# Running sums of a 31-tap depthwise convolution: a PSUM tile in place of an SBUF tile

## The chip, the cores and the metric

One core of a Trainium2 chip runs the whole program. The metric is the device time of one execution in microseconds (us). A core has five engines with a queue each, which run their own instructions in order: TensorE (PE in the profile, its weight loads PEld), VectorE (DVE), ScalarE (ACT), GpSimd (POOL) and SyncE (SP, which issues the loads here). The engines wait for each other through semaphores. Tiles lie in SBUF or in PSUM, the memory that TensorE writes its products to.

## The reference, cut to what matters

The program is a two-layer decoder trunk over 272 positions of 2048 channels. Only the first mixer of layer 0 matters here:

```python
def causal_dwconv(x, w):
    K = w.shape[0]
    L = x.shape[1]
    xp = jnp.pad(x, ((0, 0), (K - 1, 0), (0, 0)))
    out = xp[:, 0:L] * w[0]
    for t in range(1, K):
        out = out + xp[:, t:t + L] * w[t]
    return out

def mixer_ab(h, w_in, conf_dw, conf_dw_b, conf_ln_g, conf_ln_b, sc_dw, w_out):
    z = h @ w_in
    a_val, a_gate, s_b, s_c, s_x = jnp.split(z, _splits(AB_SIZES), axis=-1)
    a = a_val * jax.nn.sigmoid(a_gate)
    a = causal_dwconv(a, conf_dw) + conf_dw_b
    a = jax.nn.silu(layernorm(a, conf_ln_g, conf_ln_b))
    s = s_b * causal_dwconv(s_c * s_x, sc_dw)
    return jnp.concatenate([a, s], axis=-1) @ w_out
```

`conf_dw` has 31 taps over 1024 channels, `sc_dw` 3 taps over 1024 channels. Everything is float32.

## The kernel before, in words

Activations are kept transposed: 128 channels on the partitions, 272 positions along the free dimension. A product with a float32 weight matrix is made column by column, a column being 128 output channels (`gemm`, `gemm_steps`, lines 138 to 166). For each column, weights come in blocks of 128x512 (`wf`). ScalarE rounds a block to `wh` (L152), and the rest `wl = wf - wh` is made by a subtraction (L154), on VectorE or, for the blocks listed in `pool_lo`, on GpSimd. TensorE then does three matmuls for each 128 rows of weights (L161, L162, L163), all into one PSUM tile `acc`. A column of the input projection has 2048 rows: four blocks, 48 matmuls. In this stage `pool_lo` is `PLO = (0, 1, 2)`: three of a column's four `wl` are made by GpSimd and the last by VectorE. There are two `acc` tiles, five `wh` and five `wl`.

The input projection has 40 columns. The first 16 are eight pairs (value, gate). Of each pair, VectorE scales the two products by `rstd` (L308 `av`, L305 `ag`), ScalarE applies a sigmoid, and VectorE multiplies them into the padded tile `ap` (L311). Then the convolution of these 128 channels runs as a generator, `conv_gen`: ScalarE writes the first tap and the bias into `c` (name `conv`, L278), and VectorE adds 30 taps one by one (L280), each reading the shifted `ap`, a scalar per partition from the parameter tile `par`, and the running sum `c`, and writing `c` again. GpSimd then adds the finished channel block into `csum` (L284, L286). The other 24 columns are eight groups of three (L325 `u`, L328 `u2`, L335 `sb`), with a 3-tap convolution (`conv3`, L235 to L237).

The taps are spread over the columns: after each column `run_taps(7)` lets the generators emit seven more taps, so the 240 taps stand between the columns' other VectorE instructions. A tap is also ordered behind the last `wl` of VectorE (`behind`). A scheduler then fixes the order of each engine's queue, which may interleave the taps of two channel blocks. TensorE needs VectorE's `wl` for the last quarter of every column.

Names in PSUM: `acc` is one of two buffers, `ps` one of six (`psb()`).

Of the kernel before, what the change touches and what calls it, by code (L numbers as in the profile page):

```python
# [12 lines left out]
AF = mybir.ActivationFunctionType  # L13
ALU = mybir.AluOpType
# [7 lines left out]
T = NM + SEQ  # L22
# [14 lines left out]
PAD = 48  # L37
OUT = NM - 2

# ---------------------------------------------------------------- layout of the packed parameters  # L40
_PAR = [
    ("norm_mix0", 16), ("eps", 1), ("norm_mix1", 16), ("norm_ffn0", 16), ("norm_ffn1", 16), ("norm_final", 16),
    ("conf_dw", 31 * 8), ("conf_b", 8), ("conf_g", 8), ("conf_bb", 8), ("sc_dw", 24),
# [48 lines left out]
def _body(ctx, tc, nc, A):  # L92
    V, S, G, PE = nc.vector, nc.scalar, nc.gpsimd, nc.tensor
# [13 lines left out]
    def pc(name, i=0, r0=0, r1=P):  # L107
        o = PO[name] + i
        return par[r0:r1, o:o + 1]
# [6 lines left out]
    def psb():  # L116
        return psB.tile([P, 512], F32, tag="ps", name="ps")

    def behind(ins, others):
        for o in others:  # L120
            tc.add_manual_dep(ins.ins, o.ins.name,
                              mybir.DependencyInfo(mybir.DependencyClass.NoSync, mybir.DependencyReason.DATA),
                              reason="activation tables")
# [6 lines left out]
        if last_hi[0] is not None:  # L130
            behind(w, [*last_hi, *after])

    # ---------------------------------------------------------------- products with split operands
    side = []
    def tick():
        for t in list(side):
# [39 lines left out]
    def parts(t, c0, c1):  # L176
        return t[:, 0, c0:c1], t[:, 1, c0:c1]

    # ---------------------------------------------------------------- residual stream and its norms
    h = []  # L180

    def inv_sqrt(dst, src, scale, eps, pool=None):
# [47 lines left out]
    def add_h(m, acc, c0):  # L230
        V.tensor_add(h[m][:, c0:], h[m][:, c0:], acc)  # L231

    # ---------------------------------------------------------------- causal short convolution
    def conv3(dst, src, n, wname, i):
        S.activation(dst, src[:, 0:n], AF.Copy, scale=pc(wname, 3 * i))  # L235
        V.scalar_tensor_tensor(dst, src[:, 1:1 + n], pc(wname, 3 * i + 1), dst, op0=ALU.mult, op1=ALU.add)
        V.scalar_tensor_tensor(dst, src[:, 2:2 + n], pc(wname, 3 * i + 2), dst, op0=ALU.mult, op1=ALU.add)  # L237

    # ---------------------------------------------------------------- mixer of layer 0
    def mixer_ab(tp):  # L240
        nm = Norm("norm_mix0", 0, tp)
        h0 = tp.tile([P, KD, T], F32, name="h0", bufs=1)
# [32 lines left out]
        PLO, NT = (0, 1, 2), 7  # L275

        def conv_gen(i, c, ap):
            S.activation(c, ap[:, 0:T], AF.Identity, scale=pc("conf_dw", 31 * i), bias=pc("conf_b", i))  # L278
            for t in range(1, 31):
                tap = V.scalar_tensor_tensor(c, ap[:, t:t + T], pc("conf_dw", 31 * i + t), c, op0=ALU.mult, op1=ALU.add)  # L280
                behind(tap, last_lo)
                yield
            if i == 0:
                G.tensor_copy(csum, c)  # L284
            else:
                G.tensor_add(csum, csum, c)  # L286
# [12 lines left out]
        for i in range(8):  # L299
# [9 lines left out]
            ap = tp.tile([P, T + 30], F32, tag="apad", name="ap", bufs=4)  # L309
            V.memset(ap[:, 0:30], 0.0)  # L310
            V.tensor_mul(ap[:, 30:], av, ag)  # L311
            c = tp.tile([P, T], F32, tag="conv", name="conv", bufs=8)
# [27 lines left out]
        run_taps(240)  # L340
        warm(AF.Sqrt)

        # layer norm over the channels
        a_split = []

        def ln_gen():
# [42 lines left out]
            nxt.feed(m)  # L389
        return nxt  # L390

    # ---------------------------------------------------------------- feed-forward
    def ffn(layer, nm, gname, c1, tp, feed, spill=None):
        nxt = Norm(gname, c1, tp)
        c0 = nm.c0
        n = T - c0
        pad = 2 if layer == 0 else 0
        no = n if layer == 0 else n - 2
        xs = nm.xs()
        up, down, dw = A["up%d" % layer], A["down%d" % layer], "ffn_dw%d" % layer  # L400
        for half in range(2):
            act = []
            for j in range(NFH):
                i = half * NFH + j
                res = []
                for q in range(2):
                    ps = gemm(up, 2 * i + q, xs, n)
                    nm.finish()
                    u = tp.tile([P, T + 2], F32, tag="u%d" % q, name="u")
                    if pad:  # L410
                        G.memset(u[:, 0:2], 0.0)  # L411
                    V.tensor_mul(u[:, pad:pad + n], ps, nm.rstd)  # L412
                    c = tp.tile([P, T], F32, tag="c%d" % q, name="c")
                    conv3(c[:, :no], u, no, dw, q * NF + i)
                    res.append(c[:, :no])
                silu = S.activation(res[1], res[1], AF.Silu)  # L416
                G.tensor_mul(res[0], res[0], res[1])  # L417
                d = tp.tile([P, 2, T], F32R, tag="act", name="act", bufs=24)
                split(d, res[0], no)
                act.append(parts(d, 0, no))  # L420
            warm(AF.Sqrt, [silu])
            for m in range(KD):
                add_h(m, gemm(down, half * KD + m, act, no), T - no)
                if half:
                    feed(nxt, m)
                    if spill is not None:
                        nc.sync.dma_start(spill[:, m, :], h[m])
        return nxt
# [5 lines left out]
    with tc.tile_pool(name="ab", bufs=2) as tp:  # L434
        nm = mixer_ab(tp)
# [1 line left out]
    with tc.tile_pool(name="ffn0", bufs=2) as tp:  # L437
        nm = ffn(0, nm, "norm_mix1", 0, tp, feed_x, hs)

    # ---------------------------------------------------------------- mixer of layer 1  # L440
    H = [slice(0, 64), slice(64, 128)]

    def c5(ap):
# [2 lines left out]
    def mixer_cd(tp, nm):  # L446
# [7 lines left out]
        def ring(name):  # L454
            return hpool.tile([P, T], F32, tag="h", name=name)
# [20 lines left out]
        pctx = ExitStack()  # L476
        pp = pctx.enter_context(tc.tile_pool(name="prep", bufs=2))

        # ------------------------------------------------ low-rank input of the decay of the linear attention
        acc = psb()[:, :T]  # L480
        wf = wpool.tile([P, LOADK * P], F32, tag="wf", name="wf", bufs=NWF)[:, :KD * 32].rearrange("p (k c) -> p k c", c=32)
        nc.sync.dma_start(wf, A["glr"].rearrange("p (k c) -> p k c", c=32))
# [6 lines left out]
        for i in range(2):  # L489
            nc.sync.dma_start(gw[i], A["gw2"][:, 2 * P * i:2 * P * (i + 1)])  # L490

        # ------------------------------------------------ decay, in-context rate and key of all heads
        xt = ring("xt")
        ps24 = proj()
        nm.finish()
# [96 lines left out]
        scrN = dpool.tile([P, 32, 32], F32, name="scrN")  # L592
        scr0T = dpool.tile([16, 16, 16], F32, name="scr0T")

        # inverses of the unit triangular blocks, one block per lane
        def lanes(src, n, np_, dst, dst_n, L_, T_):
            L = L_[:np_, :n * n].rearrange("p (s t) -> p s t", s=n)
            nc.gpsimd.dma_start(L, src)
            Ti = T_[:np_, :n * n].rearrange("p (t j) -> p t j", t=n)
            G.memset(T_[:np_, :n * n], 0.0)  # L600
            G.memset(T_[:np_, 0:n * n:n + 1], 1.0)
            yield
            for s in range(n - 1):
                m, w = n - 1 - s, s + 1
                tm = pp.tile([P, 256], F32, tag="lane", name="tm")
                tv = tm[:np_, :m * w].rearrange("p (t j) -> p t j", t=m)
                G.tensor_mul(tv, Ti[:, s:s + 1, 0:w].to_broadcast([np_, m, w]),
                             L[:, s, s + 1:n].unsqueeze(2).to_broadcast([np_, m, w]))
                G.tensor_add(Ti[:, s + 1:n, 0:w], Ti[:, s + 1:n, 0:w], tv)
                if n == 32 or s % 2:  # L610
                    yield
            G.tensor_copy(L, Ti.rearrange("p t j -> p j t"))
            nc.gpsimd.dma_start(dst, L)
            if dst_n is not None:
                nc.gpsimd.dma_start(dst_n, Ti)
            yield
# [130 lines left out]
                        V.tensor_copy(lt[o:o + 32, :, 32:64], pv[o:o + 32])  # L747
                yield

        # ------------------------------------------------ gated linear attention  # L750
        groups = [(0, 16, 1), (16, 128, 2), (144, 128, 2)]
        OSP = []

# [95 lines left out]
            tick()  # L849
        pctx.close()  # L850

        # ------------------------------------------------ delta-rule recurrence, two heads at a time
        pctx = ExitStack()
        sp_ = pctx.enter_context(tc.tile_pool(name="scan", bufs=4))
        bonesr = sp_.tile([P, P], F32R, name="bonesr", bufs=1)
# [3 lines left out]
        def rw_scan(p, vp):  # L859
# [8 lines left out]
            def fill(c):  # L868
                t = sp_.tile([P, 2, P], F32, tag="arc", name="arc", bufs=4)
                cs = slice(64 * c, 64 * c + 64)  # L870
                for h0 in range(2):
                    G.tensor_copy(t[H[h0], h0].rearrange("p (a b) -> p a b", a=2), ar[H[h0], :, cs])
                return t
# [28 lines left out]
            t = fill(0)  # L902
# [8 lines left out]
            for c in range(5):  # L911
# [29 lines left out]
                if not last:  # L941
# [7 lines left out]
                    values(c + 1, nsv)  # L949
                    sv, t, g3, bt = nsv, tn, g3n, btn  # L950
                yield
            # group norm, bonus and output gate
            y = yt[:, PAD:]
            sq = sp_.tile([P, T], F32, tag="sq", name="sq", bufs=2)
            S.square(sq, y)
# [34 lines left out]
        for p in range(8):  # L990
            rt = ring("rt")
            shift(rt, p, OUT - 2)
            V.tensor_mul(AR[p][:, 1, PAD:], rt, AR[p][:, 1, PAD:])
            vp = sp_.tile([P, TP], F32, tag="vp", name="vp", bufs=4)
            V.memset(vp[:, 0:PAD], 0.0)
            shift(vp[:, PAD:], 16 + p)
            side.append(rw_scan(p, vp))
# [22 lines left out]
    with tc.tile_pool(name="cd", bufs=2) as tp:  # L1020
        nm = mixer_cd(tp, nm)
# [35 lines left out]

# ---------------------------------------------------------------- launch  # L1060
def _pack_w(w, rows, cols):
    w = w[rows[0]:rows[1]]
    k = w.shape[0]
    w = w.reshape(k // P, P, w.shape[1] // P, P)
    return np.ascontiguousarray(w[:, :, cols].transpose(2, 1, 0, 3)).reshape(len(cols), P, k)
# [77 lines left out]
```

## Time and profile before

| what | value |
|---|---|
| median of 3 runs | 2565.1 us (2564.55 to 2566.51) |
| span of the profiled execution | 2560.3 us |
| median less that span (start and end outside the records) | 4.8 us |
| PE busy, share of the span | 97% |
| DVE busy, share of the span | 73% |
| POOL busy, share of the span | 22% |
| L280, the taps | 240 instructions, 190.1 us of DVE |

The span runs from the first recorded instruction to the last. The profiled execution has only its span; what lies around it is taken from the runs. A busy share is a mean over all stages: the taps all lie in the first 290 us. Durations in the views are from an instruction's start to its recorded end; the next instruction of the engine can start some 0.08 us before that end.

### The profile page before, as it was taken

The page shows a single profiled execution, that of the slowest core. Times are in us where ns is not written, and L with a number is a line of the kernel's source. Part 1 is how long each engine was busy: PE and PEld are TensorE (multiplying, and loading weights), DVE is VectorE, ACT ScalarE, POOL GpSimd, SP SyncE. Part 2 cuts the span into 40 slices and gives each one's busy share as a digit, 9 for nine tenths or more (in the row PEclk, how much of TensorE's full clock was granted, in tenths as well). Part 3 has the DMA queues.
Part 4 walks back from the last instruction along what each step waited for, and adds up shares of the span by engine and source line. Part 5 has one row for each costly group of instructions (what it writes and reads, how often), then busy time and mean ns, then how long its engine had stood idle before and what let it go on. Part 6 is the DMA issues. An engine that isn't in the chain of part 4 may idle for free.

```text
span 2560.3 us, 53392 instructions
## 1 busy us (share of the span) xinstructions
PE 2489.4 (97%) x20476; PEld 2417.7 (94%) x20476; DVE 1859.5 (73%) x3399; ACT 1329.9 (52%) x2573; POOL 552.7 (22%) x789
## 2 busy tenths in 40 slices
PE   8888899999999999999999999999999999999998
PEld 7777899999999999999889988889999999999998
DVE  8999888767645667666787678888777755777754
ACT  5332465555544555544755445555555544555553
POOL 5565623000000000021036324324000000000022
PEclk9999999999999999999999999999999999999999
DMA  6334455555565555566444642235555566555564
GB/s 211 132 132 138 151 175 185 176 173 175 172 174 180 174 177 177 170 191 201 137 129 146 173 140 85 89 118 183 180 182 181 177 190 187 182 181 183 176 188 145
DMA packets 130350, 423.61 MB, mean 165 GB/s; under 512 B 18832, under 2 KB 26576, under 8 KB 130096
## 3 DMA queue, kind: packets, MB, share of 16 engines
q1 hardware_dynamic: 129184, 417.66, 50.9%
q0 software_dynamic: 912, 2.55, 0.4%
q8 instruction: 161, 2.64, 0.4%
q14 instruction: 93, 0.76, 0.1%
HBM read 414.09 MB, written 5.93 MB: 164 GB/s over the span
## 4 chain that ended last, share of the span: by engine, by line
PE 88%; DVE 6%; issue 3%; POOL 2%; ACT 1%; DMA 0%; SPq 0%; POOLq 0%; DVEq 0%; ACTq 0%
PE acc L161 28%; PE acc L163 27%; PE acc L162 27%; DVE conv L280 3%; POOL wl L154 2%; DVE wl L154 1%; PE ps L882 1%; PE ps L916 0%; PE ps L897 0%; PE ps L931 0%; PE ps L939 0%; PE ps L784 0%; PE ps L945 0%; PE ps L678 0%; PE ps L799 0%
## 5 line engine op out<-in xcount | busy, mean ns | idle before, releaser
L152 ACT CAST wh<-wf 128x512 fp32r<-128x512 f32 (+1 forms) x1576 | 951.7, 611 | 932.1 <-PE acc L162 829.4
L154 DVE TENSOR_TENSOR wl<-wf,wh 128x512 fp32r<-128x512 f32 (+1 forms) x1465 | 1029.2, 707 | 493.9 <-ACT wh L152 461.4
L163 PE MATMUL acc<-x,wl 128*128 128x272 f32 (+1 forms) x4224 | 1215.6, 288 | 42.0 <-DVE wl L154 30.2
L161 PE MATMUL acc<-x,wh 128*128 128x272 f32 (+1 forms) x4224 | 1224.6, 290 | 3.5 <-DVE u L325 1.8
L162 PE MATMUL acc<-x,wh 128*128 128x272 f32 (+1 forms) x4224 | 1214.9, 288 | 0.0
L163 PEld LDWEIGHTS acc<-x,wl 128*128 128x128 f32 x4224 | 795.9, 188 | 53.6 <-DVE wl L154 35.8
L161 PEld LDWEIGHTS acc<-x,wh 128*128 128x128 f32 x4224 | 798.9, 189 | 21.0 <-issue 10.9
L162 PEld LDWEIGHTS acc<-x,wh 128*128 128x128 f32 x4224 | 800.3, 189 | 1.4 <-issue 0.3
L163 PE MATMUL acc<-act,wl 128*128 128x272 f32 (+1 forms) x1408 | 401.8, 285 | 0.0
L161 PE MATMUL acc<-act,wh 128*128 128x272 f32 (+1 forms) x1408 | 401.1, 285 | 0.0
L162 PE MATMUL acc<-act,wh 128*128 128x272 f32 (+1 forms) x1408 | 399.5, 284 | 0.0
L162 PEld LDWEIGHTS acc<-act,wh 128*128 128x128 f32 x1408 | 266.6, 189 | 0.0
L161 PEld LDWEIGHTS acc<-act,wh 128*128 128x128 f32 x1408 | 265.2, 188 | 0.0
L163 PEld LDWEIGHTS acc<-act,wl 128*128 128x128 f32 x1408 | 264.7, 188 | 0.0
L417 POOL TENSOR_TENSOR c<-c 128x272 f32<-128x272 f32 (+1 forms) x88 | 66.5, 756 | 647.5 <-ACT c L416 647.4
L280 DVE SCALAR_TENSOR_TENSOR conv<-ap,par,conv 128x272 f32<-128x272 f32 x240 | 190.1, 805 | 3.5
L154 POOL TENSOR_TENSOR wl<-wf,wh 128x512 fp32r<-128x512 f32 x111 | 159.8, 1463 | 78.3 <-ACT wh L152 77.9
L411 POOL MEMSET u<- 128x2 f32 x88 | 8.5, 100 | 584.9 <-DVE c L237 572.2
L214 POOL TENSOR_TENSOR nsq<-h 128x272 f32<-128x272 f32 (+2 forms) x56 | 57.2, 1021 | 203.3 <-DVE h L231 202.0
L412 DVE TENSOR_TENSOR u<-acc,rstd 128x272 f32<-128x272 f32 (+1 forms) x176 | 76.4, 434 | 29.7 <-PE acc L163 24.9
L235 ACT ACTIVATE c<-u,par 128x272 f32<-128x272 f32 (+1 forms) x176 | 91.0, 517 | 1.9 <-DVE u L412 1.8
L237 DVE SCALAR_TENSOR_TENSOR c<-u,par,c 128x272 f32<-128x272 f32 (+1 forms) x176 | 86.9, 494 | 6.2
(306 smaller groups left out, 2307.8 us busy)
## 6 DMA issues: line engine op xcount, KB each, us to landing
wf<-up SPq DMA_DIRECT2D x352, 512.0 KB, 3.5
wf<-down SPq DMA_DIRECT2D x128, 512.0 KB, 3.7
wf<-cd_in SPq DMA_DIRECT2D x100, 512.0 KB, 3.6
wf<-ab_in SPq DMA_DIRECT2D x76, 512.0 KB, 3.6
wf<-down SPq DMA_DIRECT2D x64, 384.0 KB, 3.2
wf<-ab_out_s SPq DMA_DIRECT2D x16, 512.0 KB, 3.5
wf<-ab_out_a SPq DMA_DIRECT2D x16, 512.0 KB, 3.5
wf<-cd_out_o SPq DMA_DIRECT2D x16, 512.0 KB, 3.5
```

The source lines that it names most:

```text
L152: last_hi[0] = S.copy(wh[:, :ns * P], src)
L154: lo = eng.tensor_sub(wl[:, :ns * P], src, wh[:, :ns * P].bitcast(F32))
L161: PE.matmul(acc, a, xh, start=kk == 0, stop=False)
L162: PE.matmul(acc, a, xl, start=False, stop=False)
L163: PE.matmul(acc, b, xh, start=False, stop=kk == kt - 1)
L214: G.tensor_mul(sq[:, :n], hm, hm)
L235: S.activation(dst, src[:, 0:n], AF.Copy, scale=pc(wname, 3 * i))
L237: V.scalar_tensor_tensor(dst, src[:, 2:2 + n], pc(wname, 3 * i + 2), dst, op0=ALU.mult, op1=ALU.add)
L280: tap = V.scalar_tensor_tensor(c, ap[:, t:t + T], pc("conf_dw", 31 * i + t), c, op0=ALU.mult, op1=ALU.add)
L412: V.tensor_mul(u[:, pad:pad + n], ps, nm.rstd)
L417: G.tensor_mul(res[0], res[0], res[1])
L882: PE.matmul(gv[:, :128], bkc, t[r, h0], start=True, stop=True)
```

## The change

The running sum gets a tile of its own in PSUM. ScalarE writes the first tap and the bias there, 29 taps read it and write it back, and the last tap reads it and writes the SBUF tile `c`, which the rest of the program uses as before. The arithmetic and its order are the same. (The diff also drops comment lines elsewhere, which is left out here.)

```diff
         def conv_gen(i, c, ap):
-            S.activation(c, ap[:, 0:T], AF.Identity, scale=pc("conf_dw", 31 * i), bias=pc("conf_b", i))
+            run = psb()[:, :T]
+            S.activation(run, ap[:, 0:T], AF.Identity, scale=pc("conf_dw", 31 * i), bias=pc("conf_b", i))
             for t in range(1, 31):
-                tap = V.scalar_tensor_tensor(c, ap[:, t:t + T], pc("conf_dw", 31 * i + t), c, op0=ALU.mult, op1=ALU.add)
+                tap = V.scalar_tensor_tensor(c if t == 30 else run, ap[:, t:t + T], pc("conf_dw", 31 * i + t), run,
+                                             op0=ALU.mult, op1=ALU.add)
                 behind(tap, last_lo)
                 yield
```

With two more lines in the file, what stood at L280 stands at L281, and later lines are two higher.

The scheduler's order of TensorE's and SyncE's queues is unchanged, of ScalarE's hardly. VectorE's changes in the part of the pairs. This is one place there, before: the instructions from the `wl` ahead of one `av` to the second `wl` after it.

```order
L154 TENSOR_TENSOR wl<-wf,wh 128x512
L280 SCALAR_TENSOR_TENSOR conv<-ap,par,conv 128x272
L308 TENSOR_TENSOR av<-acc,rstd 128x272
L280 SCALAR_TENSOR_TENSOR conv<-ap,par,conv 128x272 x6
L154 TENSOR_TENSOR wl<-wf,wh 128x512
L280 SCALAR_TENSOR_TENSOR conv<-ap,par,conv 128x272
L305 TENSOR_TENSOR ag<-acc,rstd 128x272
```

The same place with the change (a last tap is the row that writes `conv`):

```order
L154 TENSOR_TENSOR wl<-wf,wh 128x512
L281 SCALAR_TENSOR_TENSOR ps<-ap,par,ps 128x272
L310 TENSOR_TENSOR av<-acc,rstd 128x272
L281 SCALAR_TENSOR_TENSOR ps<-ap,par,ps 128x272 x3
L307 TENSOR_TENSOR ag<-acc,rstd 128x272
L281 SCALAR_TENSOR_TENSOR ps<-ap,par,ps 128x272 x2
L281 SCALAR_TENSOR_TENSOR conv<-ap,par,ps 128x272
L313 TENSOR_TENSOR ap<-av,ag 128x272
L281 SCALAR_TENSOR_TENSOR ps<-ap,par,ps 128x272
L154 TENSOR_TENSOR wl<-wf,wh 128x512
```

The next `wl` has moved behind `ag` and `ap`; two rows later another follows (not shown), so that later columns are as before.

In the part of the groups VectorE's order between two `wl` stays. Before, in the sixth group:

```order
L154 TENSOR_TENSOR wl<-wf,wh 128x512
L280 SCALAR_TENSOR_TENSOR conv<-ap,par,conv 128x272
L328 TENSOR_TENSOR u_2632<-acc,rstd 128x272
L280 SCALAR_TENSOR_TENSOR conv<-ap,par,conv 128x272
L331 TENSOR_TENSOR up<-u,u_2632 128x272
L280 SCALAR_TENSOR_TENSOR conv<-ap,par,conv 128x272 x2
L236 SCALAR_TENSOR_TENSOR cv<-up,par,cv 128x272
L280 SCALAR_TENSOR_TENSOR conv<-ap,par,conv 128x272
L237 SCALAR_TENSOR_TENSOR cv<-up,par,cv 128x272
```

And with the change:

```order
L154 TENSOR_TENSOR wl<-wf,wh 128x512
L281 SCALAR_TENSOR_TENSOR ps<-ap,par,ps 128x272
L330 TENSOR_TENSOR u_2639<-acc,rstd 128x272
L281 SCALAR_TENSOR_TENSOR ps<-ap,par,ps 128x272
L333 TENSOR_TENSOR up<-u,u_2639 128x272
L281 SCALAR_TENSOR_TENSOR ps<-ap,par,ps 128x272 x2
L236 SCALAR_TENSOR_TENSOR cv<-up,par,cv 128x272
L281 SCALAR_TENSOR_TENSOR ps<-ap,par,ps 128x272
L237 SCALAR_TENSOR_TENSOR cv<-up,par,cv 128x272
```

Only the tile of the running sum is another.

## Rows read from the trace of the kernel before

**Rows 1.** The page: busy time of each engine, and the chain by line.

```profile
PE 2489.4 (97%) x20476; PEld 2417.7 (94%) x20476; DVE 1859.5 (73%) x3399; ACT 1329.9 (52%) x2573; POOL 552.7 (22%) x789
...
PE acc L161 28%; PE acc L163 27%; PE acc L162 27%; DVE conv L280 3%; POOL wl L154 2%; DVE wl L154 1%; PE ps L882 1%; PE ps L916 0%; PE ps L897 0%; PE ps L931 0%; PE ps L939 0%; PE ps L784 0%; PE ps L945 0%; PE ps L678 0%; PE ps L799 0%
```

**Rows 2.** Busy time in four stretches: window, length, then busy us (instructions) by engine.

```profile
core 0: us, PE busy (x) PEld busy (x) DVE busy (x) ACT busy (x) POOL busy (x), PEclk, DMA share, GB/s
36.98:153.00 116.02, 98.02 (x724) 94.57 (x722) 114.09 (x164) 40.17 (x73) 66.04 (x47) 0.96 0.39 136
...
430.00:530.00 100.00, 100.00 (x799) 100.00 (x798) 71.06 (x128) 54.87 (x101) 7.86 (x25) 1.00 0.53 177
...
153.00:288.02 135.02, 110.80 (x819) 103.83 (x818) 133.33 (x190) 44.02 (x84) 77.46 (x56) 1.00 0.40 131
288.02:312.96 24.94, 24.36 (x193) 24.14 (x193) 13.13 (x20) 12.36 (x22) 16.18 (x12) 1.00 0.63 205
```

**Rows 3.** Waits from 37 to 313 us: total us, times, longest.

```profile
POOL wl L154 <- ACT wh L152: 76.7, 29, 5.7
...
PE acc L163 <- DVE wl L154: 28.7, 20, 6.7
...
POOL csum L286 <- DVE conv L280: 25.1, 7, 4.8
...
PE acc L163 <- POOL wl L154: 11.6, 16, 1.5
```

**Rows 4.** The taps' line: shortest, median and longest duration in ns.

```profile
L280 DVE SCALAR_TENSOR_TENSOR conv<-ap,par,conv x240: 480/502/1543, 37.9 to 287.1; 128x272 f32<-128x272 f32 x120
```

**Rows 5.** VectorE's groups from 37 to 153 us: busy us, mean ns of one.

```profile
L280 DVE SCALAR_TENSOR_TENSOR conv<-ap,par,conv 128x272 f32<-128x272 f32 x122 | 93.9, 793 | 1.8
L154 DVE TENSOR_TENSOR wl<-wf,wh 128x512 fp32r<-128x512 f32 x15 | 15.6, 1043 | 0.0
L311 DVE TENSOR_TENSOR ap<-av,ag 128x272 f32<-128x272 f32 x8 | 4.3, 540 | 1.5 <-ACT ag L306 1.5
```

**Rows 6.** VectorE's groups from 153 to 288 us.

```profile
L280 DVE SCALAR_TENSOR_TENSOR conv<-ap,par,conv 128x272 f32<-128x272 f32 x119 | 97.4, 822 | 1.7
L154 DVE TENSOR_TENSOR wl<-wf,wh 128x512 fp32r<-128x512 f32 x18 | 17.7, 982 | 0.0
L237 DVE SCALAR_TENSOR_TENSOR cv<-up,par,cv 128x272 f32<-128x272 f32 x6 | 9.2, 1526 | 0.0
L331 DVE TENSOR_TENSOR up<-u,u 128x272 f32<-128x272 f32 x6 | 4.8, 799 | 0.0
...
L336 DVE TENSOR_TENSOR sb<-sb,cv 128x272 f32<-128x272 f32 x6 | 2.6, 432 | 0.0
L335 DVE TENSOR_TENSOR sb<-acc,rstd 128x272 f32<-128x272 f32 x6 | 2.6, 431 | 0.0
```

**Rows 7.** VectorE in order of time, 58.7 to 65.8 us: start, length, what.

```profile
58.62 7.28 DVE L280 SCALAR_TENSOR_TENSOR conv<-ap,par,conv 128x272 f32<-128x272 f32 x5
```

**Rows 8.** GpSimd in the same stretch, with the idle time before.

```profile
58.16 7.43 POOL L154 TENSOR_TENSOR wl<-wf,wh 128x512 fp32r<-128x512 f32 x5 [5.20 <-ACT wh L152]
```

**Rows 9.** VectorE from 65.9 to 69.2 us: taps of two channel blocks in turn, a `wl`.

```profile
65.82 3.37 DVE L280 SCALAR_TENSOR_TENSOR conv<-ap,par,conv 128x272 f32<-128x272 f32 x8
69.12 0.68 DVE L154 TENSOR_TENSOR wl<-wf,wh 128x512 fp32r<-128x512 f32 x1
```

**Rows 10.** VectorE from 243.75 to 245.73 us, taps of one channel block.

```profile
243.71 2.12 DVE L280 SCALAR_TENSOR_TENSOR conv<-ap,par,conv 128x272 f32<-128x272 f32 x4
```

**Rows 11.** Line 652, which reads one SBUF tile, `par` and PSUM.

```profile
L652 DVE SCALAR_TENSOR_TENSOR kn<-kc,par,ps x8: 483/492/498, 1299.0 to 1338.8; 128x272 f32<-128x272 f32 x8
```

**Rows 12.** VectorE from 1324.65 to 1325.04 us.

```profile
1324.64 0.49 DVE L652 SCALAR_TENSOR_TENSOR kn<-kc,par,ps 128x272 f32<-128x272 f32 x1
```

**Rows 13.** GpSimd in the same stretch.

```profile
1324.34 1.02 POOL L667 TENSOR_TENSOR kt<-kt,kc 128x272 f32<-128x272 f32 x1
```

**Rows 14.** Busy time from 64 to 72.5 us, columns as in rows 2.

```profile
64.00:72.50 8.50, 2.65 (x11) 2.65 (x12) 8.50 (x18) 0.20 (x1) 1.59 (x2) 0.69 0.20 64
```

## The prediction

> **What bounds the kernel now.** Start with the page. TensorE is busy for 97% of the span, and the chain that ended last is its matmuls at 82%; VectorE's taps hold 3% of it and `wl` another 3% [rows 1]. So almost everywhere nothing but fewer or faster matmuls would help. Next look for the stretch where that is not so, in the table of stretches [rows 2]. Late in the program TensorE issues 799 matmuls of this shape in 100 us with no idle time: 0.1252 us each, a column of 48 in 6.01 us. That is its pace. From 36.98 to 153.00 us it issues 724 in 116.02 us, which at its pace take 90.6: 25.4 us are lost. From 153.00 to 288.02 it issues 819 in 135.02, at its pace 102.5: 32.5 lost. From 288.02, where the taps end, to 312.96 it loses 0.8. Together 58.7 us, and no more can be won here.
>
> Who holds it back? In the first two stretches VectorE is busy 114.09 of 116.02 and 133.33 of 135.02 us [rows 2]: it has no time left. The waits say the same: TensorE waited 28.7 us for VectorE's `wl`, and 11.6 for GpSimd's [rows 3]. GpSimd's waits for `wh` are no cause of their own, since ScalarE's queue stands behind results of VectorE.
>
> Why is VectorE full? The taps take 93.9 and 97.4 us of it [rows 5, 6]. Their durations have two levels: median 502 ns, longest 1543 [rows 4], mean 793 and 822. The timeline shows when which holds. From 58.62 us five taps take 7.28 us, 1.46 each, while GpSimd makes five `wl` in 7.43, 1.49 each [rows 7, 8]: the two take turns. Straight after, with GpSimd idle, eight taps take 3.37 us, about 0.41 from start to start [rows 9]. So a tap that meets a GpSimd instruction loses about 1 us. I take 0.495 us for one that doesn't.
>
> **The change part by part.** *Does a tap with its sum in PSUM still meet GpSimd?* The nearest instruction is line 652: the same operation and size, one SBUF tile, a scalar from `par`, the other tile from PSUM. All eight take 483 to 498 ns [rows 11], one of them wholly inside a GpSimd instruction that reads two SBUF tiles: 1324.64 to 1325.13 within 1324.34 to 1325.36 [rows 12, 13]. An instruction with two SBUF tiles in the same stage is stretched: L237 takes 1526 ns on the mean [rows 6]. So I expect that a tap takes 0.495 us whatever GpSimd does.
>
> *What VectorE saves.* First stretch: 122 x (0.793 - 0.495) = 36.4 us. Second: 119 x (0.822 - 0.495) = 38.9 us (one of the 240 taps stands in both windows) [rows 5, 6]. VectorE then has 114.1 - 36.4 = 77.7 us of work against TensorE's 90.6, and 133.3 - 38.9 = 94.4 against 102.5. In both TensorE becomes the slower one.
>
> *Reading PSUM* costs nothing that the rows show: L335, with one operand in PSUM, takes 431 ns, L336 with both in SBUF 432 [rows 6]; line 652 takes as long as an unblocked tap [rows 4, 11].
>
> [...]
>
> *Writing PSUM* no VectorE instruction of this trace does, so it is bounded. Below: nothing more than a write to SBUF. A gain would have to come out of the 0.41 us from start to start; no row where only the memory differs shows VectorE faster by more than 10 ns, so I leave it out. Above: the write can't overlap the read. An element costs (0.68 - 0.43)/(512 - 272) = 1.04 ns, from an unblocked `wl` [rows 9] and L335 [rows 6]; a second pass over 272 elements adds 0.28 us, 0.78 for a tap. I take 0.01 us, near the lower end: TensorE adds into 272 columns of a PSUM buffer every 0.125 us [rows 2], so the memory takes a read and a write much faster than VectorE asks for them.
>
> *The extra tile.* `run` takes one of the six `ps` buffers. By then the first three hold products and sums long read; from the fourth channel block on, a buffer comes round whose user ended a block earlier. No wait. ScalarE's first taps now write PSUM; they are eight instructions in 250 us, and I count nothing for them. The last tap writes SBUF with one SBUF tile read, so it is not stretched either, and GpSimd's `csum` finds its tile as before. The 25.1 us that GpSimd waits there now [rows 3] shrink with faster taps.
>
> *The order.* TensorE's and SyncE's queues are unchanged. VectorE's moves some `wl` by a few taps in the pairs' part. I cost it at nothing: the five `wl` buffers let VectorE run nearly a column ahead, and its 90.6 - 77.7 = 12.9 us of slack there cover it. Without that cover, a `wl` that stands three taps later costs TensorE 3 x 0.41 = 1.2 us.
>
> *What remains lost.* First stretch, 3 us: at the start 17 taps stand between two `wl` (13 of them are those of rows 7 and 9), with two other instructions of 0.43 us and a `wl` of 0.68, each beginning 0.08 before the last one's end: 17 x 0.41 + 2 x 0.35 + 0.60 = 8.3 us against a column's 6.0. [...] Second stretch, 5 us: VectorE's 94.4 of 102.5 leave little, and `cv`, `up` and `wl` still read two SBUF tiles. Third stretch 0.8. The write, 241 x 0.01 = 2.4 us of VectorE, mostly in idle time: 0.9. Together 9.7, so the gain is 58.7 - 9.7 = 49 us. After 313 us TensorE is at its pace, and the gain reaches the end. Loads must bring a column, 1 MB, every 6.01 us, 174 GB/s; the later stage gets 177 [rows 2]. The span becomes 2560.3 - 49 = 2511.3. The median of the runs shown lies 4.8 above the span, which is what surrounds it: **2516 us**.
>
> **The rivals.**
>
> *A: as above, 2516*; by itself 2507 (2 us lost instead of 9.7) to 2525.
>
> *B: the waits move to GpSimd.* GpSimd's instructions come in bursts [rows 8], and VectorE's with two SBUF tiles may meet more of them. TensorE's 11.6 us of waits for GpSimd's `wl` stay [rows 3]. Today's loss of VectorE in the second stretch is 6 x 1.03 (L237) + 6 x 0.37 (L331) + 18 x 0.30 (`wl`) = 13.8 us [rows 6]; doubled, it needs 94.4 + 13.8 = 108.2 against 102.5, 5.7 too much. Gain 49 - 11.6 - 5.7 = 32: 2533. For it: L237 is stretched in the mean of all six. Against it: GpSimd is idle for 43% of that stretch [rows 2].
>
> *C: an access to PSUM is dearer by a fixed amount.* Second stretch: VectorE falls behind from (102.5 - 94.4)/119 = 0.068 us a tap on. Half of the bound, 0.14 us: 119 x 0.14 - 8.1 = 8.6 too much there, and in the first 77.7 + 122 x 0.14 - 90.6 = 4.2. Gain 36: 2529. For it: a row on the write is missing. Against it: the rows on the read. [...]
>
> *D: the write doesn't overlap the read.* A tap takes 0.78 us: VectorE saves 122 x 0.013 + 119 x 0.042 = 6.6 us. 2558. Against it: the matmuls' pace above.
>
> *E: slower.* As D, and a tap starts only when the one before it has landed in PSUM, whichever channel block that belongs to. Taps of one block in a row do so today: four take 2.12 us, 0.53 from start to start, 0.04 after the end [rows 10]; of two blocks in turn they don't (0.41 [rows 9]). Then 0.78 + 0.04 = 0.82 from start to start, against 190.1/240 = 0.79 (the page's total for the taps) today: 240 x 0.03 = 7 us more, 2572. It decides from 0.79 us a tap on. Against it: all that speaks against D.
>
> *F: nothing changes.* The scalar from `par` lies in SBUF too and might count as the second input; then taps still meet GpSimd, 2565. Against it: line 652 has that scalar as well [rows 11 to 13].
>
> **How the numbers follow.** A 0.58, B 0.17, C 0.12, D 0.04, E 0.05, F 0.04. The range is A's lower end, 2507, to beyond B, 2540; it leaves out D, E, F and some edges of A and C, 0.18 together. A measurement of this kernel tells 0.2% (5 us) from no change. Faster by more than that: A to D, 0.91; within: F, 0.04; slower by more: E, 0.05.
>
> **What would show it.** Right: L281's longest duration close to its median of 0.5 us, VectorE's busy time in the taps' stage some 70 us lower, GpSimd's `wl` shorter than 1.49 us, and the last column of the input projection ending near 264 us instead of 313. B: taps at 0.5 us, but TensorE's waits for GpSimd's `wl` over 15 us. C: all taps at one level of 0.55 to 0.65 us. D or E: all near 0.8. F: two levels as before. Wrong, too, if TensorE then stands behind ScalarE, whose queue waits for `up` and `sb`.

## The result, and the profile after

The median of the changed kernel is 2505.9 us (2504.4 to 2508.4, four runs), against 2564.8 (2563.0 to 2566.5) of the kernel before on the same chip: a ratio of 0.9768 (95% interval 0.9757 to 0.9780). That is 58.9 us faster, where 49 were forecast; the time lies 1.1 us below the lower end of the range.

The page of the profiled execution (2504.39 us, span 2502.6), its busy times and the chain that ended last, beside [rows 1]:

```profile
PE 2474.0 (99%) x20476; PEld 2412.9 (96%) x20476; DVE 1785.1 (71%) x3399; ACT 1337.6 (53%) x2573; POOL 539.2 (22%) x789
...
PE acc L161 31%; PE acc L162 30%; PE acc L163 30%; PE ps L884 1%; PE ps L918 1%; PE ps L899 0%; PE ps L933 0%; PE ps L941 0%; PE ps L786 0%; DMA h<-hT 0%; PE ps L947 0%; PE ps L680 0%; DVE wl L154 0%; PE ps L801 0%; PE ps L799 0%
```

VectorE's taps have left the chain, and with them most of `wl`. VectorE is busy for 1859.5 - 1785.1 = 74.4 us less, with the same 3399 instructions.

The table of stretches answers to [rows 2]. The first two windows hold the same 724 and 819 matmuls as there, the third the last four columns of the input projection, the fourth what follows:

```profile
37.66:128.22 90.56, 90.56 (x724) 90.56 (x723) 81.96 (x169) 44.82 (x77) 61.66 (x49) 1.00 0.52 175
128.22:230.68 102.46, 102.46 (x819) 102.46 (x818) 92.05 (x185) 47.05 (x80) 71.73 (x56) 1.00 0.53 178
230.51:254.78 24.27, 24.27 (x195) 24.27 (x194) 11.92 (x19) 12.62 (x22) 12.27 (x9) 1.00 0.57 187
254.85:350.00 95.15, 93.30 (x741) 92.97 (x740) 84.95 (x128) 58.27 (x106) 36.19 (x38) 1.00 0.52 169
```

In the first three TensorE is busy for the whole window, at a granted clock of 1.00. 90.56 and 102.46 us are the 90.6 and 102.5 that its matmuls need at its pace: nothing that counts is lost between 37.66 and 254.78 us. All of the columns there take 6.03 us from end to end. Before, this work ran from 36.98 to 312.96, 275.98 us; now it takes 217.12, so 58.9 us are won here, which is the whole gain. VectorE is busy for 82.0 of 90.6 and 92.1 of 102.5 us: it is now the faster of the two, by some 10%.

All the taps, beside [rows 4], with least, median and longest duration in ns:

```profile
L281 DVE SCALAR_TENSOR_TENSOR ps<-ap,par,ps x232: 489/499/509, 38.6 to 224.4; 128x272 f32<-128x272 f32 x116
L281 DVE SCALAR_TENSOR_TENSOR conv<-ap,par,ps x8: 485/492/498, 63.1 to 225.2; 128x272 f32<-128x272 f32 x8
```

One level is left; the longest fell from 1543 to 509 ns. The waits from 37 to 255 us answer to [rows 3] (us in total, times, longest):

```profile
ACT wh L152 <- PE acc L162: 99.5, 121, 0.9
POOL wl L154 <- ACT wh L152: 57.3, 78, 1.7
DVE wl L154 <- ACT wh L152: 25.3, 17, 4.7
...
POOL csum L288 <- DVE conv L281: 2.7, 2, 1.4
POOL csum L286 <- DVE conv L281: 2.6, 1, 2.6
```

TensorE waits for no `wl` any more, neither of VectorE nor of GpSimd. The direction has turned: ScalarE's casts wait for TensorE, and VectorE waits 25.3 us for casts, up to 4.7 at a time. It has run ahead of TensorE until it has no buffer left. GpSimd's `wl`, from the view of line 154, are shorter too, median 1297 ns instead of 1482, and in the timeline they stand one by one instead of in bursts as in [rows 8]:

```profile
L154 POOL TENSOR_TENSOR wl<-wf,wh x111: 1285/1297/1748, 29.3 to 246.4; 128x512 fp32r<-128x512 f32 x111
```

VectorE's groups from 128 to 231 us, beside [rows 6]:

```profile
L281 DVE SCALAR_TENSOR_TENSOR ps<-ap,par,ps 128x272 f32<-128x272 f32 x113 | 56.1, 500 | 1.5
L154 DVE TENSOR_TENSOR wl<-wf,wh 128x512 fp32r<-128x512 f32 x18 | 15.3, 851 | 8.6 <-ACT wh L152 8.6
L237 DVE SCALAR_TENSOR_TENSOR cv<-up,par,cv 128x272 f32<-128x272 f32 x5 | 5.8, 1154 | 0.0
L333 DVE TENSOR_TENSOR up<-u,u 128x272 f32<-128x272 f32 x5 | 5.5, 1104 | 0.0
...
L337 DVE TENSOR_TENSOR sb<-acc,rstd 128x272 f32<-128x272 f32 x6 | 2.6, 432 | 0.0
```

What still reads two SBUF tiles (`wl`, `cv`, `up`) is still stretched: `wl` to 851 ns on the mean, where the one of [rows 9] took 0.68 us, `up` more than before (1104 ns on the mean instead of 799), L237 less (1154 instead of 1526). It costs nothing now, since VectorE has time to spare.

One thing is left near the stage: the first column of the next product takes 5.58 us from end to end instead of 3.01. It waits 1.8 us for VectorE's `ssp`, and did so before the change in the same way (1.8 us; 5.57 from end to end).

### The profile page after: what moved, and what is told of

Its sections match the earlier page's. It is cut to its first block, busy times and chain, and to the rows that moved or that the text cites. A ratio compares the mean times of both kernels' runs of the same rounds, so it can differ in the third digit from the quotient of the medians.

```text
span 2502.6 us, 53391 instructions
## 1 busy us (share of the span) xinstructions
PE 2474.0 (99%) x20476; PEld 2412.9 (96%) x20476; DVE 1785.1 (71%) x3399; ACT 1337.6 (53%) x2573; POOL 539.2 (22%) x789
## 4 chain that ended last, share of the span: by engine, by line
PE 97%; DVE 1%; DMA 1%; ACT 0%; issue 0%; POOL 0%; SPq 0%; DVEq 0%; ACTq 0%; POOLq 0%
PE acc L161 31%; PE acc L162 30%; PE acc L163 30%; PE ps L884 1%; PE ps L918 1%; PE ps L899 0%; PE ps L933 0%; PE ps L941 0%; PE ps L786 0%; DMA h<-hT 0%; PE ps L947 0%; PE ps L680 0%; DVE wl L154 0%; PE ps L801 0%; PE ps L799 0%
## 5 line engine op out<-in xcount | busy, mean ns | idle before, releaser
L161 PEld LDWEIGHTS acc<-x,wh 128*128 128x128 f32 x4224 | 797.2, 189 | 17.3 <-issue 7.5
L154 POOL TENSOR_TENSOR wl<-wf,wh 128x512 fp32r<-128x512 f32 x111 | 148.0, 1339 | 59.5 <-ACT wh L152 58.5
L281 DVE SCALAR_TENSOR_TENSOR ps<-ap,par,ps 128x272 f32<-128x272 f32 x232 | 112.1, 500 | 3.0
L414 DVE TENSOR_TENSOR u<-acc,rstd 128x272 f32<-128x272 f32 (+1 forms) x176 | 76.4, 434 | 29.5 <-PE acc L163 24.7
L237 DVE SCALAR_TENSOR_TENSOR c<-u,par,c 128x272 f32<-128x272 f32 (+1 forms) x176 | 86.9, 494 | 6.2
```

The source lines that it names most:

```text
L154: lo = eng.tensor_sub(wl[:, :ns * P], src, wh[:, :ns * P].bitcast(F32))
L161: PE.matmul(acc, a, xh, start=kk == 0, stop=False)
L281: tap = V.scalar_tensor_tensor(c if t == 30 else run, ap[:, t:t + T], pc("conf_dw", 31 * i + t), run, op0=ALU.mult, op1=ALU.add)
```

## The experiments

They fall in two parts. The first four ask whether it is the second SBUF tile that made the taps slow. The other six ask why no part of the forecast 9.7 us was lost. In them, the *lead* of a `wl` of VectorE is the time from its end to the start of the first matmul that reads it (the 39th of a column's 48).

### The padded input in PSUM instead of the sum

Starting from the kernel before; the sums stay in SBUF.

```diff
-            ap = tp.tile([P, T + 30], F32, tag="apad", name="ap", bufs=4)
+            ap = psb()[:, :T + 30]
```

> The kernel before with the padded input `ap` in PSUM instead and the running sum in SBUF, as it was. Theory (a tap is slow when it and GpSimd both read SBUF twice, so one SBUF tile less in the tap is enough, whichever it is): all taps at 0.48 to 0.52 us, no loss of TensorE in the stage, ratio to before 0.977 (2506 us). Rival (it is the sum's place that counts, for instance because a dependent tap gets its sum back sooner from PSUM): two levels of 0.49 and 1.4 us as before, ratio 0.99 to 1.00.

Measured: 2506.5 us (2505.1 to 2508.5), ratio 0.9775 (0.9760 to 0.9789). All the taps, in the view of their line:

```profile
L280 DVE SCALAR_TENSOR_TENSOR conv<-ps,par,conv x240: 484/494/504, 40.1 to 226.9; 128x272 f32<-128x272 f32 x120
```

It is not the running sum that matters, but that one of the two tiles is not in SBUF, whichever. These taps write SBUF and take 494 ns, those of the change write PSUM and take 499 (medians): the write to PSUM costs some 5 ns.

### GpSimd writes and doesn't read

The kernel before, taps and sums in SBUF. In the input projection GpSimd fills its `wl` with zeros instead of subtracting, which leaves out the low parts of three blocks in four there.

```diff
-                lo = eng.tensor_sub(wl[:, :ns * P], src, wh[:, :ns * P].bitcast(F32))
+                if eng is G:
+                    lo = G.memset(wl[:, :ns * P].bitcast(F32), 0.0)
+                else:
+                    lo = eng.tensor_sub(wl[:, :ns * P], src, wh[:, :ns * P].bitcast(F32))
```

> The kernel before, its taps in SBUF; GpSimd's subtractions are replaced by a memset of `wl`, which writes SBUF and reads nothing (the low parts of three in four weight blocks of the input projection are left out). Theory (GpSimd's reads hold up a VectorE instruction with two SBUF tiles): taps at 0.49 us, all of them, with nothing in PSUM; VectorE's busy time in the stage falls by 75 us or more; ratio 0.976 to 0.978. Rival (any GpSimd instruction in SBUF holds it up): taps still on two levels, the upper one shorter as the memset is; ratio 0.98 to 1.00.

Measured: 2504.2 us (2502.8 to 2504.6), ratio 0.9764 (0.9749 to 0.9779). The taps, and GpSimd's instructions from 37 to 255 us in the view by groups:

```profile
L283 DVE SCALAR_TENSOR_TENSOR conv<-ap,par,conv x240: 483/496/1020, 37.0 to 223.8; 128x272 f32<-128x272 f32 x120
```

```profile
L155 POOL MEMSET wl<- 128x512 f32 x105 | 55.2, 526 | 144.6 <-PE acc L166 144.6
L289 POOL TENSOR_TENSOR csum<-csum,conv 128x272 f32<-128x272 f32 x7 | 6.0, 851 | 2.4 <-DVE conv L283 2.3
```

GpSimd still writes 105 tiles of 128x512, and the taps with two SBUF tiles take 496 ns. They do meet these writes: 170 of the 240 taps overlap a `MEMSET` and nothing else of GpSimd, and they take 484 to 505 ns. The only two taps over 506 ns, 1020 and 648, each overlap an instruction for `csum`, which still reads. What holds a tap up here is a GpSimd instruction that *reads* SBUF while the tap reads two tiles there. Two traces show it: in the kernel before, where GpSimd subtracts, 81 of the 91 taps that overlap one of its subtractions take over 600 ns, and no other tap does; in this run those that meet only writes take 505 at most.

### One half of the channel blocks at a time

The change for the first four channel blocks alone, then for the last four alone.

```diff
-            run = psb()[:, :T]
+            run = psb()[:, :T] if i < 4 else c
```

> The change for the first four of eight channel blocks only; the others keep their sum in SBUF. Theory (each stretch ends at the pace of the slower of VectorE and TensorE): the first stretch wins its 25.4 us, the second keeps its loss of 32.5: span 2535, ratio 0.990. Rival (one slow block spoils the whole, or half is enough, through the buffers): ratio 0.998 or 0.980.

```diff
-            run = psb()[:, :T]
+            run = psb()[:, :T] if i >= 4 else c
```

> The change for the last four of eight channel blocks only. Theory (stretch by stretch): the second stretch wins 32.5 us, the first keeps 25.4 lost: span 2528, ratio 0.987. With the run on the first half the two gains should add up to that of the whole change, 58 us. Rival: the sum of the two gains is over 70 or under 45 us.

Measured: 2537.5 us (2535.2 to 2540.2), ratio 0.9892 (0.9875 to 0.9908), and 2534.1 (2532.2 to 2536.5), ratio 0.9882 (0.9867 to 0.9897), both against 2563.6 of the kernel before on that chip. The gains are 26.1 and 29.5 us, near the 25.4 and 32.5 that the two stretches had lost; their sum, 55.6, is near the 58.9 of the whole. With the first half changed, the stretches to 128 us and from there:

```profile
37.00:128.00 91.00, 91.00 (x722) 91.00 (x721) 78.92 (x166) 44.52 (x75) 61.27 (x49) 0.99 0.48 170
128.00:288.00 160.00, 139.48 (x1034) 133.68 (x1033) 147.52 (x210) 57.41 (x106) 95.38 (x68) 0.98 0.41 142
```

Each half repairs its own stretch; nothing is handed on to the next.

### More work for VectorE, spread out

The changed kernel, with further instructions of a tap's shape whose result nobody reads: 32 in all (`t % 7`), then 112 (`t % 2`).

```diff
                 behind(tap, last_lo)
+                if t % 7 == 0 and t < 30:
+                    junk = tp.tile([P, T], F32, tag="junk", name="junk", bufs=1)
+                    more = V.scalar_tensor_tensor(junk, ap[:, t:t + T], pc("conf_dw", 31 * i + t), run, op0=ALU.mult, op1=ALU.add)
+                    behind(more, last_lo)
                 yield
```

> The change, and four more VectorE instructions of a tap's form for each channel block (32 in all, reading `ap` and the sum, writing a tile that nobody reads). VectorE was busy 82.0 of 90.6 and 92.1 of 102.5 us in the two stretches. Theory (as long as VectorE's work is below TensorE's, the `wl` made ahead hide it entirely): 16 x 0.41 = 6.6 us more in each stretch still fit, at most 1.5 us lost, ratio to before 0.977 to 0.978. Rival (the prediction's own step: near full load a part is lost anyway, 5 us of a stretch at 92%): 5 to 10 us lost, ratio 0.979 to 0.982.

> As the run with 32 more instructions, with 14 for each channel block, 112 in all. Theory: 56 x 0.41 to 0.54 = 23 to 30 us more in each stretch, over TensorE's pace by 14 to 22 and 13 to 20 us: 27 to 42 us lost, ratio 0.987 to 0.994. VectorE is then busy for over 98% of the stage again, with taps still at 0.5 us. Rival (something other than VectorE sets the pace of this stage now): under 20 us lost.

Measured with 32: 2507.2 us (2504.8 to 2508.2), ratio 0.9770 (0.9755 to 0.9784). No loss, and every column takes 6.03 us but one (6.05), though VectorE has 32 x 0.41 = 13 us less to spare. The stage, from the fifth column to the last:

```profile
42.05:259.20 217.15, 217.15 (x1731) 217.15 (x1730) 200.38 (x403) 101.83 (x177) 149.68 (x113) 1.00 0.51 176
```

With 112: 2525.5 (2520.6 to 2531.9), ratio 0.9844 (0.9827 to 0.9862), some 20 us lost. That is less than the 27 to 42 forecast, and by its size it falls to the rival (under 20). The trace has to decide. Its stage as a whole, then the part of it that loses nothing, then what TensorE waits for VectorE's `wl` in it (us in total, times, longest):

```profile
41.97:274.45 232.48, 221.70 (x1732) 220.41 (x1731) 221.73 (x467) 102.80 (x178) 146.01 (x112) 0.99 0.47 161
41.97:132.50 90.53, 90.53 (x724) 90.53 (x722) 85.33 (x185) 44.58 (x77) 60.83 (x48) 1.00 0.47 167
```

```profile
PE acc L163 <- DVE wl L154: 9.1, 4, 2.8
```

The expectation's reckoning, the sum of VectorE's work over a stretch, failed: VectorE is not busy for 98% of the stage but for 221.7 of 232.5 us, and the first 90.5 us hold 45 of the 112 instructions and lose nothing: only 98 of the 240 taps stand in them, where the changed kernel has 124 in its first 90.6 us, so taps were put off to later columns.

The rival fails too, for it is VectorE's `wl` that TensorE waits for, in four places. There two `wl` end 9.4, 13.5, 12.1 and 11.6 us apart, and the lead of the first of the two is 0.6, 4.8, 3.3 and 0.6. What is left of each distance after a column of 6.03 and that lead is 2.8, 2.6, 2.7 and 5.0 us; these four columns are 2.6, 2.3, 2.9 and 5.1 longer than 6.03 (the last of them also waits 1.4 for an `acc` buffer that VectorE has yet to read). Two columns that follow are 1.4 and 1.1 longer, and the others are not, 15.4 us in all.

### The same 32 instructions in one place

```diff
+                if i == 2 and t == 15:
+                    for _ in range(32):
+                        junk = tp.tile([P, T], F32, tag="junk", name="junk", bufs=1)
+                        more = V.scalar_tensor_tensor(junk, ap[:, t:t + T], pc("conf_dw", 31 * i + t), run, op0=ALU.mult, op1=ALU.add)
+                        behind(more, last_lo)
+                    burst[:] = [more]
...
                 if eng is V:
                     last_lo[0] = lo
+                    behind(lo, burst)
```

> The changed kernel, with 32 more instructions of a tap's shape on VectorE (sum in PSUM read, result into an unused SBUF tile), all in one place, in the middle of the third channel block, and the next wl behind them. It is the same amount of work as the 32 that stood apart, which cost nothing. In the changed kernel's trace a wl of VectorE ends at most 4.81 us before TensorE needs it, and about 0.5 of that is left when it is just in time, so VectorE can fall 4.3 us behind. Theory (the lead covers what is uneven, up to its length): 32 x 0.41 = 13.1 us more between two wl, less the 0.8 us or so by which a column's VectorE work is shorter than 6.03 there, less 4.3: about 8 us lost, in one or two columns beside the place and in no other; 2514, ratio near 0.980. Rival (only the stage's sum of work decides): nothing lost, 2506, ratio 0.977, all columns 6.03. Rival of the prediction (uneven work is lost whole, whatever the lead): 12 us or more lost, 2518, ratio 0.982.

Measured: 2522.9 us (2519.9 to 2525.5), ratio 0.9839 (0.9825 to 0.9852). The same instructions that cost nothing when spread cost 16 to 18 us in one place, so the sum of work does not decide. But the expected 8 us were too few, and by its time alone the run would count for the third answer on record, that uneven work is lost whole (12 us or more). The trace has to decide. VectorE around the place, in order of time, and then TensorE:

```profile
79.51 1.08 DVE L155 TENSOR_TENSOR wl<-wf,wh 128x512 fp32r<-128x512 f32 x1
...
84.51 2.10 DVE L289 SCALAR_TENSOR_TENSOR junk<-ap,par,ps 128x272 f32<-128x272 f32 x4
...
88.52 14.35 DVE L289 SCALAR_TENSOR_TENSOR junk<-ap,par,ps 128x272 f32<-128x272 f32 x27
...
103.20 0.68 DVE L155 TENSOR_TENSOR wl<-wf,wh 128x512 fp32r<-128x512 f32 x1
```

```profile
91.26 0.29 PE L165 MATMUL acc<-x,wl 128*128 128x272 f32 x1
103.94 0.59 PE L165 MATMUL acc<-x,wl 128*128 128x272 f32 x1 [12.39 <-DVE wl L155]
```

Twenty-seven of them take 14.35 us, 0.53 from start to start and not 0.41; each has to wait in the program for a semaphore that VectorE's own instructions raise. Even 32 x 0.53 = 17 us would have fitted into the time that VectorE is idle in this stage (8.6 + 10.4 + 12.4 = 31.4 us in the table of stretches). One `wl` ends at 80.59 us, the next at 103.88: 23.29 between them, 17.3 more than a column. The first of the two had a lead of 4.39. By the theory TensorE should then wait 17.3 - 4.4 = 12.9 us; it waits 12.4. By the third answer it would have been 17.3. So the lead is taken off at its full length, and the expectation's 8 us came mostly from the wrong duration. The rest of the loss is the clock. The stretches of the wait and after it:

```profile
91.00:103.45 12.45, 0.55 (x5) 0.32 (x3) 11.67 (x25) 0.50 (x1) 0.35 (x1) 0.64 0.00 0
103.45:113.00 9.55, 9.06 (x57) 9.07 (x58) 8.47 (x18) 2.64 (x5) 3.88 (x3) 0.76 0.67 212
113.00:264.00 151.00, 151.00 (x1205) 151.00 (x1204) 124.90 (x247) 71.27 (x120) 104.64 (x81) 1.00 0.50 175
```

After the wait 57 matmuls take 9.06 us instead of 57 x 0.1252 = 7.1, at a granted clock of 0.76, so 1.9 us more. 12.4 + 1.9 = 14.3 of the 14.5 by which the stage is longer (from 38.02 to 269.62, 231.6 us, where the changed kernel takes 217.1). The span is 16.2 longer; the other 1.7 lie outside the stage, most of them behind it, and what caused them is open.

### Fewer buffers, and so a shorter lead

The changed kernel with four, two and three `wh` and `wl` buffers in the columns of the input projection; all run in this order.

```diff
-                wh = wpool.tile([P, SUB * P], F32R, tag="wh", name="wh")
-                wl = wpool.tile([P, SUB * P], F32R, tag="wl", name="wl")
+                pool, nb = few[0]
+                wh = pool.tile([P, SUB * P], F32R, tag="wh", name="wh", bufs=nb)
+                wl = pool.tile([P, SUB * P], F32R, tag="wl", name="wl", bufs=nb)
...
+        few[0] = (tp, 4)
```

> The change with four `wh` and four `wl` buffers for the input projection instead of five (they come from the stage's own pool; later stages keep five). A smaller lead of VectorE. Theory (the lead hides the uneven spread of VectorE's work over the columns; with four it is still over 3 us): 0 to 2 us lost against the change. Rival (the lead plays no part): nothing lost here nor with fewer.

> The change with two `wh` and two `wl` buffers for the input projection. Theory (lead): VectorE and GpSimd can begin a `wl` only when TensorE is done with the block two before it, so nearly no lead is left, and each column in which VectorE's instructions between two `wl` take over 6 us loses the excess; 15 us or more lost against the change. Rival (the mean load of VectorE alone decides): under 3 us lost.

> The changed kernel with three wh and three wl buffers in the columns of the input projection instead of five; the work is the same. In the traces so far the wl of VectorE ended at most 4.81 us before its use with five buffers, 3.39 with four, 0.8 with two, and with four it fell to 0.62 in the worst place without a loss. Theory (the buffers make the lead, and the lead covers uneven work): a lead of about 2 us at most, columns at or within 0.3 us of 6.03 where VectorE's work is even, and waits of TensorE for VectorE's wl of 1 to 3 us in the few places where two wl stand 8 to 10 us apart: 5 to 20 us lost, 2511 to 2526, ratio 0.979 to 0.985. Rival (the sum of work alone decides): at most 0.1 us per column, under 4 us lost, ratio below 0.9785. Other cause to look for, as with two buffers: a uniformly longer column with waits for GpSimd's wl, which would say nothing of VectorE's lead.

| `wh`, `wl` buffers | longest lead | least lead | longest between two `wl` | us | ratio |
|---|---|---|---|---|---|
| 5 (the change) | 4.81 | 0.48 | 9.60 | 2505.9 | 0.9768 (0.9757 to 0.9780) |
| 4 | 3.39 | 0.62 | 8.85 | 2504.2 | 0.9762 (0.9748 to 0.9777) |
| 3 | 1.82 | 0.05 | 7.69 | 2508.9 | 0.9788 (0.9774 to 0.9801) |
| 2 | 1.32, mostly 0.8 | 0.05 | 9.26 | 2547.9 | 0.9931 (0.9914 to 0.9947) |

The leads are read from the trace, from the fifth column to the 39th. Buffers make the lead, as the theory says. With four each column takes 6.08 us instead of 6.03 for a cause that is open, 1.9 us in all, and the median shows no loss. With three some 3 us are lost (2.7 in the stage), and not 5 to 20; the ratio lies between the two forecasts, and its interval reaches into both. The reason is in the fourth column of the table. The scheduler makes its order anew for each kernel, and with four and three buffers it puts the `wl` at more even distances, with three 7.69 us at most. 7.69 less a column of 6.08 is 1.6, which a lead of 1.82 covers. In one place the lead doesn't cover it: at a lead of 0.54 the next `wl` comes 7.45 us after the last, 0.9 too late, and TensorE waits 0.8. So this run fits the lead, but puts it to little test, since with the buffers the order changed too. Nor is the run with two a test: it lost 42 us, as the expectation has it (15 or more), but evenly, some 7.06 us in nearly every column, and in another place. The waits from 37 to 262 us:

```profile
DVE wl L156 <- ACT wh L154: 33.6, 18, 3.7
PEld acc L165 <- POOL wl L156: 31.0, 61, 1.1
...
PE acc L165 <- POOL wl L156: 17.8, 61, 0.9
```

TensorE waits 61 times for GpSimd's `wl`, and VectorE for casts. With two buffers the way from cast to GpSimd to matmul is too long for the column; that reading comes from the waits and was not tested by itself.

## Why the prediction was right, and where it was wrong

**What bounds the kernel: right.** The prediction's ceiling of 58.7 us, matmuls at their pace in the two stretches of the taps and the one after, is what was won (58.9 in the stage, 58.9 between the medians). The halves each gave nearly their own stretch.

**A tap's time: right.** 0.499 us for 0.495, whatever GpSimd does. VectorE saved 74.4 us in all for 75.3; in the two stretches it is busy for 174.0 us where 77.7 + 94.4 = 172.1 was worked out.

**Reading and writing PSUM: right.** Neither costs anything that counts: 499 ns with a PSUM tile read and written, 494 with one read, 496 with none (medians, the last from the run in which GpSimd only writes). L337 takes 432 ns, 431 before the change. Rivals C, D and E fall with this; B falls with TensorE's waits for GpSimd, which are gone, and F with the taps' single level.

**The order: right.** The moved `wl` cost nothing. The stall and the granted clock of 0.69 of [rows 14] are gone; over the same microseconds, 64 to 72.5, it is 1.00. The 0.69 is a mean: the granted clock was 0.77 from 64 to 70 us, which is the stall, and 0.50 in the 2.5 us after it.

**What remains lost: wrong.** This step charged 3 us to the first stretch, 5 to the second, 0.8 to the third and 0.9 for the write, 9.7 in all; the runs show none of it. In the first stretch it took a place where VectorE has more to do between two `wl` than a column lasts, and counted the excess as lost. The 5 us of the second were put there without a reckoning, because VectorE was nearly full. But VectorE runs ahead, as the prediction itself says in the step on the order, and what it is ahead covers the excess. The place that was priced at 8.3 against 6.0 us is in the changed kernel this one (VectorE in order of time, in two pieces, and the matmul):

```profile
49.64 0.68 DVE L154 TENSOR_TENSOR wl<-wf,wh 128x512 fp32r<-128x512 f32 x1
...
58.88 1.04 DVE L154 TENSOR_TENSOR wl<-wf,wh 128x512 fp32r<-128x512 f32 x1
```

```profile
60.52 0.29 PE L163 MATMUL acc<-x,wl 128*128 128x272 f32 x1
```

The two `wl` end at 50.32 and 59.92 us, 9.60 apart, even more than was forecast. The first was 4.17 us ahead of its matmul (at 54.49, a column of 6.03 ahead of 60.52), so the second is still 4.17 - (9.60 - 6.03) = 0.60 ahead of its own. Nothing waits. Two columns later the lead is back at 3.55, after a `wl` that comes only 2.96 us after the last. The 32 instructions that cost nothing apart and 12.4 us of wait in one place show the rule, and so do the four places of the run with 112: a loss begins where the excess is more than the lead, and is near the difference.

Without this step the sum would have been 2560.3 - 58.7 + 4.8 = 2506.4 us, against 2505.9 measured. The range could not hold that: its lower end, 2507, is given as 2 us lost, which by the same sum are 2508.4, and nothing lost is 0.6 below it.

**The 4.8 us: misread, without harm.** They are not what surrounds the span. A run's time and its own span lie 1.8 us apart (2504.39 and 2502.6 after the change); the other 3.0 are that the profiled execution of the kernel before was that much faster than the median. The sum takes the gain off the median all the same.

## What to carry to other kernels

Where an engine feeds another through a ring of buffers, don't price each uneven stretch by itself. Write down how far ahead the feeder is, take each excess off that lead, give each shortfall back up to what the buffers hold, and count a loss only from where it is used up. Where VectorE shares a stage with GpSimd, look for its instructions that read two SBUF tiles while GpSimd reads SBUF: moving either operand to PSUM, or letting GpSimd only write, freed the taps here (medians of 499, 494 and 496 ns, where 81 of 240 had taken over 600), and it matters as long as VectorE, and not TensorE, is the slower one.

## What the runs showed of the hardware that was not expected

A write of 272 columns to PSUM by VectorE costs hardly more than one to SBUF (499 and 494 ns), which no row before showed. Instructions in a row that write the same tile start 0.53 us apart, though none reads what the one before wrote (`junk`, 27 in 14.35 us); a tap behind one of the 112 that stand apart starts 0.40 to 0.42 after it (six of them, 149 to 161 us). In the program each of the 27 waits for a semaphore of VectorE's own that the one before raises; whether the engine alone would be faster is not shown. And a wait of TensorE of 12.4 us cost more than itself: the granted clock was 0.64 in it and 0.76 in the 9.55 us after, where 57 matmuls took 1.9 us longer. In the kernel before it was 0.50 in the 2.5 us after the stall of 64 to 70 us, with 11 matmuls.
